# Stick-breaking heads of an encoder layer: the strict mask as one more TensorE product per query block, and |z| on ScalarE

## The chip, the cores and the metric

The kernel runs on one core of one Trainium2 chip. The metric is the device time of one execution in microseconds (us). The engines of the core are named as the profile names them: PE (TensorE matmul), PEld (TensorE weight load), DVE (VectorE), ACT (ScalarE), POOL (GpSimd) and SP (SyncE, which only issues transfers here).

## What is computed

One encoder layer on 512 tokens of width 2048: a norm, one projection to queries, keys and values of three groups of attention heads, the three kinds of attention, an output projection with a residual, then a gated MLP with a short causal convolution, a second residual and a last norm. The change touches the second group only, eight stick-breaking heads of width 64:

```python
z = jnp.einsum('bhqd,bhkd->bhqk', q_blk, k).astype(jnp.float32) * scale
causal = k_pos[None, :] < q_pos[:, None]
log_1m_beta = jnp.where(causal, -jax.nn.softplus(z), 0.0)
suffix = lax.cumsum(log_1m_beta, axis=3, reverse=True) - log_1m_beta
log_a = jax.nn.log_sigmoid(z) + suffix
a = jnp.where(causal, jnp.exp(log_a), 0.0).astype(v.dtype)
return jnp.einsum('bhqk,bhkd->bhqd', a, v)
```

So both the softplus and the weight of a key at or after the query have to come out as zero.

## The kernel before, in words

**Tiling.** Tokens stand in four blocks of 128. Every fp32 operand of a large product is split into a high and a low part of type fp32r (a cast on ACT, line 59, and a subtraction on DVE, line 60), and a product is three matmuls (`mm3`, lines 63 to 66). Weights come in units of 128 x 2048 through SP, are split in halves of 128 x 1024, and the halves live in three buffers (`wspl`), so that the cast of a new half waits until PE has read the old one.

**Heads.** There are sixteen head steps n = 0 to 15: n = 0 to 7 are differential heads, n = 8 to 11 are pairs of stick-breaking heads (`stick_pair`), n = 12 to 15 are pairs of band heads. `weave` (line 608) writes PE's order by hand: it lets the head step n yield small pieces and puts between them the matmuls of `following(n)`, which are the projections of the next head (`project_head`, banks q and k) and part of the values of a later one (`values_unit`, bank v). PE runs in exactly that order. The order on ACT, DVE and POOL is chosen by a planner, once, when the kernel is built; on the chip each engine then works its list strictly in order.

**A stick pair before the change** (lines 513 to 557). For each of the two heads c = 0, 1: four query blocks i = 3, 2, 1, 0 of scores, each from two matmuls into a PSUM bank (`block_scores`, lines 352 to 358), copied by ACT into z (line 536; a tile of 128 x 1280 that holds the four blocks' lower triangle, with the diagonal block last in each). Then a chain over that tile, in which every step needs the one before:

- line 540, DVE: l = min(-z, z), which is -|z|
- lines 541 and 542, ACT: l = exp(l), then l = ln(1 + l)
- line 543, DVE: l = max(z, 0) + l, the softplus
- line 518 with l, POOL: in each of the four diagonal blocks, l = 0 where the key is not before the query
- line 548, DVE: four scans from the right, one per query block
- line 549, DVE: z = z - l
- line 518 with z, POOL: z = -3e38 in the same places
- line 551, ACT: z = exp(z)

After both heads the generator yields `SB_WAIT` = 28 units, so that PE gets that much of the other matmuls. Then PE transposes the first head's z (line 388, tile `tr`), ACT and DVE split the transposes into rh and rl (lines 59 and 60), the same follows for the second head, and the products with the values (lines 402 and 403, bank `pv`) and the head norm end the step.

**Temporaries.** Bias tiles of the differential and the band heads share two buffers (tag `bias`): `dist` takes the first and serves until head step 7; `rbias` (line 493, loaded by POOL's queue) takes them in turn for the band heads. Other temporaries of 128 x 512 share six buffers (tag `t2`).

Of the kernel before, what the change touches and what calls it, by code (L numbers as in the profile page):

```python
# [8 lines left out]
F32 = mybir.dt.float32  # L9
F32R = mybir.dt.float32r  # L10
AF = mybir.ActivationFunctionType
ALU = mybir.AluOpType
# [3 lines left out]
P = 128  # L16
S = 512
D = 2048
KT = D // P
NB = S // P  # L20
# [3 lines left out]
NCH = NFT // CH  # L24
NSEV = 32
NEG = -3.0e38
SB_WAIT = 28
NORM_EPS = 1e-6
SUBLN_EPS = 1e-5
# [13 lines left out]
def trunk(ctx, tc, xT, wqkv, wo, wo15, wgu, wd, par, lam4, rel, out):  # L43
    nc = tc.nc
    sync, act, dve, pool, pe = nc.sync, nc.scalar, nc.vector, nc.gpsimd, nc.tensor
# [37 lines left out]
    def acc_bank(name="acc"):  # L83
        return ps_acc.tile([P, S], F32, tag="acc", name=name)

    def att_bank(name="att"):
        return ps_att.tile([P, S], F32, tag="att", name=name)
# [42 lines left out]
    ident = const.tile([P, P], F32, name="ident")  # L130
# [80 lines left out]
    def constants(tmp, khigh):  # L211
# [11 lines left out]
        dve.scalar_tensor_tensor(out=dist, in0=dist, scalar=-1.0, in1=dist, op0=ALU.mult, op1=ALU.min)  # L223
        dve.memset(dist[0:HD, S - HD : S], NEG)
        scr = tmp.tile([P, S], F32, tag="t2", name="scr")
# [15 lines left out]
    with ExitStack() as actx:  # L241
        qk = actx.enter_context(tc.tile_pool(name="qk", bufs=2))
        vp = actx.enter_context(tc.tile_pool(name="vp", bufs=4))
        tmp = actx.enter_context(tc.tile_pool(name="tmp", bufs=6))
# [104 lines left out]
            return (p[:, 0 : 2 * P], 2) if j == NB - 1 else (p[:, PAD + OFF[j] : PAD + OFF[j] + WID[j]], j)  # L349


        def block_scores(qkh, c, i, bank):


            q, k, kh = qkh
            qt, kt = slice(i * P, (i + 1) * P), slice(0, max(i + 1, 2) * P)
            pe.matmul(bank[:, kt], q[c][:, qt], k[c][:, kt], start=True, stop=False)  # L357
            pe.matmul(bank[:, kt], q[c][:, qt], kh[c][:, kt], start=False, stop=True)  # L358

        UOFF = [0, 128, 384, 768]  # L360

        def softmax_block(qkh, c, i, bias, dst, sums, n):
# [11 lines left out]
                scale=1.0,  # L374
                scalar=NEG,
                accum_out=mx,
# [4 lines left out]
        def transposed(w):  # L381

            (ph, pl), p = parts()
            for j in reversed(range(NB)):
                bank = att_bank("tr")
                for i in range(j, NB):
                    o = UOFF[i] + j * P
                    pe.transpose(out=bank[:, (i - j) * P : (i - j + 1) * P], in_=w[:, o : o + P], identity=ident)  # L388
                t = slice(OFF[j], OFF[j] + WID[j])
                split(ph[:, t], pl[:, t], bank[:, 0 : WID[j]])  # L390
                yield 1
            return p
# [87 lines left out]
        def pair_out(vs, p0, p1, gain, slot):  # L480
            v = vs()
            o, ct = o_tile(), tmp.tile([P, S], F32, tag="t2", name="ct")
            values_pair(0, v, p0, ct, o)
            yield 2
            values_pair(1, v, p1, ct, o)
            yield 1
            yield from finish(o, pair1, HD, NORM_EPS, gain, slot)

        def chunk_pair(p, qkh, vs):
            ws = []  # L490
            for c in range(2):
                bias = tmp.tile([P, S], F32, tag="bias", name="rbias", bufs=2)
                pool.dma_start(bias, rel[2 * p + c])
                dve.memset(bias[0:HD, S - HD : S], NEG)
                w = f5.tile([P, TRI], F32, tag="f5", name="w")
# [15 lines left out]
            yield from pair_out(vs, p0, p1, pt[:, C_CH + p : C_CH + p + 1], 12 + p)  # L511

        def stick_pair(p, qkh, vs):
            def strictly_before(t, fill):

                for i in range(NB):
                    o = UOFF[i] + i * P
                    pool.affine_select(  # L518
                        out=t[:, o : o + P],
                        in_=t[:, o : o + P],  # L520
                        pattern=[[-1, P]],
                        compare_op=ALU.is_gt,
                        fill=fill,
                        base=0,
                        channel_multiplier=1,
                    )

            zs = []
            for c in range(2):
                z = f5.tile([P, TRI], F32, tag="f5", name="z")  # L530
                zs.append(z)
                for i in reversed(range(NB)):
                    w = (i + 1) * P
                    bank = att_bank("z")
                    block_scores(qkh, c, i, bank)
                    act.copy(out=z[:, UOFF[i] : UOFF[i] + w], in_=bank[:, 0:w])
                    yield 1

                l = f5.tile([P, TRI], F32, tag="f5", name="l")
                dve.scalar_tensor_tensor(out=l, in0=z, scalar=-1.0, in1=z, op0=ALU.mult, op1=ALU.min)  # L540
                act.activation(l, l, AF.Exp)
                act.activation(l, l, AF.Ln, bias=1.0)
                dve.scalar_tensor_tensor(out=l, in0=z, scalar=0.0, in1=l, op0=ALU.max, op1=ALU.add)
                strictly_before(l, 0.0)
                for i in reversed(range(NB)):

                    back = l[:, UOFF[i] : UOFF[i] + (i + 1) * P][:, ::-1]
                    dve.tensor_tensor_scan(back, back, back, 0.0, ALU.add, ALU.max)  # L548
                dve.tensor_tensor(out=z, in0=z, in1=l, op=ALU.subtract)
                strictly_before(z, NEG)  # L550
                act.activation(z, z, AF.Exp)
            yield SB_WAIT
            p0 = yield from transposed(zs[0])
            yield 6
            p1 = yield from transposed(zs[1])
            yield 1
            yield from pair_out(vs, p0, p1, pt[:, C_SB + p : C_SB + p + 1], 8 + p)


        TOTAL = {diff_head: 30, stick_pair: 33 + SB_WAIT, chunk_pair: 39}  # L560
        NH, HEADS_AT = 16, 16
        ready, vtiles, pending = {}, {}, []

        def unit_order():
            yield from (HEADS_AT, HEADS_AT + 1)
# [23 lines left out]
        def nxt():  # L589

            load_next()
            return ahead.pop(0)
# [5 lines left out]
        def following(n):  # L598

            yield from project_head(n + 1, nxt)  # L600
            m, s = (n + 2) // 2, n % 2
            if s == 0:
                vbanks[:] = [acc_bank("v0"), acc_bank("v1")]
            yield from values_unit(m, s, vbanks, nxt())
            if s == 1:
                vtiles[m] = values_out(m, vbanks)

        def weave(n, others, count, lead=0, slack=0, last=True):
            att, total = head(n)
            done, emitted = 0, lead  # L610
            for _ in range(lead):
                next(others)
            for w in att:
                done += w
                while emitted < count and (emitted - lead) * (total + slack) < done * (count - lead):
                    emitted += 1
                    next(others, None)
            for _ in others if last else ():
                pass
# [46 lines left out]
        input_scale_columns()  # L666
        vtiles[0] = values_out(0, vbanks)
        for n in range(NH - 2):
            weave(n, following(n), 48, 8 if n == 0 else 0)
        last = first_outputs()  # L670
        weave(NH - 2, last, 46, last=False)
# [14 lines left out]
    with ExitStack() as actx:  # L686
# [19 lines left out]
        for m in range(KT):  # L706
            if m < 4:
                bank = wo_banks[m]
            else:
                bank = acc_bank("wo")  # L710
# [277 lines left out]
    with ExitStack() as actx:  # L988
# [237 lines left out]
        with tc.manual_schedule(engines={E.PE, E.DVE, E.Activation, E.SP, E.Pool}):  # L1226
# [4 lines left out]
            for s in range(len(units) * NSTEP + 3):  # L1231
                u, k = divmod(s, NSTEP)
                if u < len(units):
                    v, q = divmod(s + 1, NSTEP)
# [166 lines left out]
```

## Time and profile before

| | us |
|---|---|
| median of three timed runs | 2220.88 (2220.15 to 2222.6) |
| the profiled execution, its own time | 2223.95 |
| its span, first to last instruction | 2222.2 |
| PE busy in the span | 2176.9 (98%) |
| PEld / DVE / ACT / POOL busy | 1984.2 / 1614.7 / 1060.1 / 324.1 |
| stretch of the four stick pairs | 375 to 555 |

The profile is one execution. Its first part gives the busy time of each engine. A view by windows gives the same for stretches of the span, with the clock granted to TensorE as a share of 2.4 GHz. A view of waits says which instruction sat idle until which other ended. A timeline lists instructions by engine with their start and length, and in brackets the idle time before them and what ended it. A busy PE is not a PE at its peak, since matmuls overlap; what one matmul costs is read from the start of it to the start of the next.

### The profile page before, as it was taken

Reading aid. Unit: us, or ns where it says so; the run is one execution under the profiler, and the core shown is the slowest. Engines: PE = TensorE matmul, PEld = TensorE weight load, DVE = VectorE, ACT = ScalarE, POOL = GpSimd, SP = SyncE. Lnnn points to the kernel's source line nnn. Section 1 sums busy time; section 2 is a strip of 40 time slices with the busy share of each in tenths; the row PEclk is TensorE's granted clock in tenths of the full one; section 3 lists DMA queues with packets and bytes.
Section 4 is the critical chain, followed back from the end, with each engine's and each line's share of the span. In section 5 each row is a group of like instructions: output and inputs, shape, how many; then the busy total and the mean of one; then the engine's idle time right before and its main releaser. Section 6 shows DMA issues by size and latency. Waiting matters only on the chain.

```text
span 2222.2 us, 34979 instructions
## 1 busy us (share of the span) xinstructions
PE 2176.9 (98%) x13884; PEld 1984.2 (89%) x13884; DVE 1614.7 (73%) x2283; ACT 1060.1 (48%) x1558; POOL 324.1 (15%) x593
## 2 busy tenths in 40 slices
PE   8999999989999999989999999999999999999997
PEld 7889898878888888889999999999999978888887
DVE  6665666787777546877777777777777778887675
ACT  5555555565566333344444444444444554544232
POOL 0100101221110321112111111111111110000003
PEclk9999999999999999999999999999999999999999
DMA  5332434222234544778778877787777565655742
GB/s 199 104 115 100 123 101 125 84 80 76 86 117 141 187 145 164 257 233 242 196 218 220 211 222 221 191 239 217 195 187 205 206 235 194 213 199 220 273 170 77
DMA packets 98164, 388.15 MB, mean 175 GB/s; under 512 B 11408, under 2 KB 20368, under 8 KB 81040
## 3 DMA queue, kind: packets, MB, share of 16 engines
q1 hardware_dynamic: 65728, 269.90, 35.7%
q0 software_dynamic: 30976, 114.84, 20.2%
q8 instruction: 109, 1.79, 0.3%
q10 hardware_dynamic: 1296, 1.17, 0.2%
q14 instruction: 55, 0.45, 0.1%
HBM read 341.30 MB, written 52.95 MB: 177 GB/s over the span
## 4 chain that ended last, share of the span: by engine, by line
PE 87%; DVE 5%; DMA 3%; ACT 2%; issue 2%; POOL 1%; SPq 0%; POOLq 0%; DVEq 0%; ACTq 0%
PE c L66 36%; PE r L66 12%; PE wo L66 8%; PE v L66 8%; PE q L66 6%; PE k L66 6%; PE dn L66 6%; PE tr L388 1%; DMA f<-t_dram 1%; PE pv L66 1%; PE sc L358 1%; PE sc L357 1%; DVE l L548 1%; POOL z L518 1%; DMA xt<-x_dram 1%
## 5 line engine op out<-in xcount | busy, mean ns | idle before, releaser
L60 DVE TENSOR_TENSOR wl<-a,wh 128x1024 fp32r<-128x1024 f32 x199 | 243.4, 1223 | 176.2 <-ACT wh L59 176.0
L66 PE MATMUL c<-bl,wh 128*128 128x256 f32 x1280 | 363.6, 284 | 4.7 <-ACT wh L59 4.7
L66 PE MATMUL c<-bh,wl 128*128 128x256 f32 x1280 | 363.5, 284 | 2.3 <-DVE wl L60 2.3
L66 PE MATMUL c<-bh,wh 128*128 128x256 f32 x1280 | 363.3, 284 | 0.0
L59 ACT CAST wh<-a 128x1024 fp32r<-128x1024 f32 x199 | 209.0, 1050 | 243.4 <-DVE a L862 206.6
L59 ACT CAST wh<-raw 128x1024 fp32r<-128x1024 f32 (+1 forms) x163 | 168.6, 1035 | 257.4 <-PE wo L66 85.1
L66 PE MATMUL c<-h2l,wh 128*128 128x256 f32 x960 | 272.0, 283 | 1.4 <-DVE U L888 0.9
L66 PE MATMUL c<-h2h,wl 128*128 128x256 f32 x960 | 271.8, 283 | 0.0
L66 PE MATMUL c<-h2h,wh 128*128 128x256 f32 x960 | 271.8, 283 | 0.0
L66 PEld LDWEIGHTS c<-bl,wh 128*128 128x128 f32 x1280 | 246.9, 193 | 4.9 <-ACT wh L59 4.9
L66 PEld LDWEIGHTS c<-bh,wl 128*128 128x128 f32 x1280 | 246.8, 193 | 2.6 <-DVE wl L60 2.6
L66 PEld LDWEIGHTS c<-bh,wh 128*128 128x128 f32 x1280 | 246.8, 193 | 0.0
L60 DVE TENSOR_TENSOR wl<-raw,wh 128x1024 fp32r<-128x1024 f32 (+1 forms) x163 | 197.6, 1214 | 65.6 <-ACT wh L59 64.9
L66 PEld LDWEIGHTS c<-h2l,wh 128*128 128x128 f32 x960 | 184.4, 192 | 1.8 <-DVE U L888 1.1
L66 PEld LDWEIGHTS c<-h2h,wl 128*128 128x128 f32 x960 | 184.4, 192 | 0.0
L66 PEld LDWEIGHTS c<-h2h,wh 128*128 128x128 f32 x960 | 184.4, 192 | 0.0
L66 PE MATMUL r<-wl,fh 128*128 128x512 f32 x448 | 174.8, 390 | 2.3 <-DVE wl L1129 2.3
L66 PE MATMUL r<-wh,fh 128*128 128x512 f32 x448 | 174.4, 389 | 0.0
L66 PE MATMUL r<-wh,fl 128*128 128x512 f32 x448 | 174.3, 389 | 0.0
L66 PE MATMUL v<-wl,hh 128*128 128x256 f32 x512 | 149.3, 292 | 9.5 <-DVE wl L60 9.2
L66 PE MATMUL v<-wh,hl 128*128 128x256 f32 x512 | 147.2, 287 | 0.4 <-DVE hl L170 0.4
L66 PE MATMUL v<-wh,hh 128*128 128x256 f32 x512 | 147.0, 287 | 0.0
(301 smaller groups left out, 5204.9 us busy)
## 6 DMA issues: line engine op xcount, KB each, us to landing
a<-in_wgu SPq DMA_DIRECT2D x121, 512.0 KB, 5.9
raw<-in_wd SPq DMA_DIRECT2D x48, 1024.0 KB, 5.8
raw<-in_wqkv SPq DMA_DIRECT2D x46, 1024.0 KB, 4.8
z<-in_wgu SPq DMA_DIRECT2D x80, 512.0 KB, 5.5
z<-in_wgu POOLq DMA_DIRECT2D x78, 512.0 KB, 9.5
raw<-in_wo SPq DMA_DIRECT2D x16, 1024.0 KB, 4.8
raw<-in_wgu SPq DMA_DIRECT2D x8, 1024.0 KB, 4.8
ab_dram<-g POOLq DMA_DIRECT2D x32, 256.0 KB, 6.3
```

Source lines behind the costliest of these rows:

```text
L59: a = act.copy(out=hi, in_=src)
L60: d = dve.tensor_tensor(out=lo, in0=src, in1=hi.bitcast(F32), op=ALU.subtract)
L66: pe.matmul(o, l[x], r[y], start=start and i == 0, stop=stop and i == 2, skip_group_check=on)
L357: pe.matmul(bank[:, kt], q[c][:, qt], k[c][:, kt], start=True, stop=False)
L358: pe.matmul(bank[:, kt], q[c][:, qt], kh[c][:, kt], start=False, stop=True)
L388: pe.transpose(out=bank[:, (i - j) * P : (i - j + 1) * P], in_=w[:, o : o + P], identity=ident)
L518: pool.affine_select(out=t[:, o : o + P], in_=t[:, o : o + P], pattern=[[-1, P]], compare_op=ALU.is_gt, fill=fill, base=0, channel_multipl ...
L548: dve.tensor_tensor_scan(back, back, back, 0.0, ALU.add, ALU.max)
```

## The change

The mask is made once, before head step 7 (`far_masks`): a 128 x 128 identity and a 128 x 256 tile whose left half is zero and whose right half holds -2^127 where the key is not before the query, both in fp32r. `block_scores` gets a third matmul for the stick heads, identity times mask, which adds the mask to the last 256 columns of the block's scores (128 columns for block 0). A masked score is then about -1.7e38: its |z| gives exp(-|z|) = 0, ln(1 + 0) = 0 and max(z, 0) = 0, so its softplus is 0, and exp(z - l) is 0. The two POOL selections per head (`strictly_before`) go. -|z| on DVE becomes |z| on ACT, and the minus moves into the scale of the exponential.

```diff
+FAR = -(2.0**127)
...
-        def block_scores(qkh, c, i, bank):
+        def block_scores(qkh, c, i, bank, strict=False):
...
             pe.matmul(bank[:, kt], q[c][:, qt], k[c][:, kt], start=True, stop=False)
-            pe.matmul(bank[:, kt], q[c][:, qt], kh[c][:, kt], start=False, stop=True)
+            pe.matmul(bank[:, kt], q[c][:, qt], kh[c][:, kt], start=False, stop=not strict)
+            if strict:
+
+                w = P if i == 0 else 2 * P
+                kt = slice((i + 1) * P - w, (i + 1) * P)
+                pe.matmul(bank[:, kt], far[0], far[1][:, 2 * P - w :], start=False, stop=True)
...
-            def strictly_before(t, fill):
-
-                for i in range(NB):
-                    o = UOFF[i] + i * P
-                    pool.affine_select(
-                        out=t[:, o : o + P],
...
-                block_scores(qkh, c, i, bank)
+                block_scores(qkh, c, i, bank, True)
...
-                dve.scalar_tensor_tensor(out=l, in0=z, scalar=-1.0, in1=z, op0=ALU.mult, op1=ALU.min)
-                act.activation(l, l, AF.Exp)
+                act.activation(l, z, AF.Abs)
+                act.activation(l, l, AF.Exp, scale=-1.0)
                 act.activation(l, l, AF.Ln, bias=1.0)
                 dve.scalar_tensor_tensor(out=l, in0=z, scalar=0.0, in1=l, op0=ALU.max, op1=ALU.add)
-                strictly_before(l, 0.0)
...
                 dve.tensor_tensor(out=z, in0=z, in1=l, op=ALU.subtract)
-                strictly_before(z, NEG)
                 act.activation(z, z, AF.Exp)
...
+        def far_masks():
+
+            t = tmp.tile([P, S], F32R, tag="bias", name="far", bufs=2)
+            b = tmp.tile([P, S], F32, tag="t2", name="diagonal")
+            pool.memset(b[:, 0 : 2 * P], 0.0)
+            pool.affine_select(
+                out=b[:, P : 2 * P],
+                in_=b[:, P : 2 * P],
+                pattern=[[-1, P]],
+                compare_op=ALU.is_gt,
+                fill=FAR,
+                base=0,
+                channel_multiplier=1,
+            )
+            dve.tensor_copy(t[:, 0:P], ident)
+            dve.tensor_copy(t[:, P : 3 * P], b[:, 0 : 2 * P])
+            far[:] = t[:, 0:P], t[:, P : 3 * P]
...
         for n in range(NH - 2):
+            if n == 7:
+                far_masks()
             weave(n, following(n), 48, 8 if n == 0 else 0)
```

## Rows read from the trace of the kernel before

**Rows 1.** First part of the page: busy us (share of the span) x instructions.

```profile
PE 2176.9 (98%) x13884; PEld 1984.2 (89%) x13884; DVE 1614.7 (73%) x2283; ACT 1060.1 (48%) x1558; POOL 324.1 (15%) x593
```

**Rows 2.** Windows: stretch, length, busy us of each engine (instructions), granted clock, DMA, GB/s.

```profile
375.00:555.00 180.00, 168.21 (x962) 147.63 (x962) 140.98 (x195) 110.47 (x193) 40.42 (x89) 0.97 0.25 82
555.00:665.00 110.00, 110.00 (x636) 96.33 (x635) 79.89 (x209) 66.84 (x153) 15.75 (x41) 1.00 0.28 98
880.00:955.00 75.00, 68.05 (x321) 57.03 (x320) 62.83 (x94) 31.25 (x35) 7.93 (x15) 0.96 0.82 268
```

**Rows 3.** Waits within 375 to 556: total us, times, longest.

```profile
ACT z L551 <- POOL z L518: 35.0, 8, 8.5
...
PE tr L388 <- ACT z L551: 10.0, 4, 2.8
...
PE pv L402 <- DVE rl L60: 1.1, 1, 1.1
```

**Rows 4.** Timeline of PE: start, us, instruction, idle time before it and its releaser.

```profile
400.36 0.33 PE L388 MATMUL tr<-ident,z 128*128 128x128 f32 x1 [2.15 <-ACT z L551]
...
452.51 0.55 PE L388 MATMUL tr<-ident,z 128*128 128x128 f32 x3 [2.81 <-ACT z L551]
...
490.84 0.33 PE L388 MATMUL tr<-ident,z 128*128 128x128 f32 x1 [2.22 <-ACT z L551]
...
543.61 0.90 PE L388 MATMUL tr<-ident,z 128*128 128x128 f32 x3 [2.81 <-ACT z L551]
```

**Rows 5.** Windows around the last two of these, columns as in the second group.

```profile
491.50:495.50 4.00, 4.00 (x17) 3.35 (x16) 3.40 (x5) 2.99 (x7) 1.97 (x4) 0.57 0.02 4
542.50:550.00 7.50, 6.39 (x31) 6.39 (x32) 5.69 (x10) 6.76 (x13) 0.00 (x0) 0.54 0.33 128
```

**Rows 6.** Timeline of DVE, POOL and ACT: end of the chain, head step 8, c = 0.

```profile
393.70 1.49 DVE L549 TENSOR_TENSOR z<-z,l 128x1280 f32<-128x1280 f32 x1
...
396.03 2.97 POOL L518 TENSOR_SCALAR_AFFINE_SELECT z<-z 128x128 f32<-128x128 f32 x4
...
399.03 1.27 ACT L551 ACTIVATE z<-z 128x1280 f32<-128x1280 f32 x1 [8.42 <-POOL z L518]
```

**Rows 7.** The same timelines: head step 9, chain of c = 1, and a weight cast.

```profile
433.99 1.05 ACT L59 CAST wh<-raw 128x1024 fp32r<-128x1024 f32 x1 [4.23 <-PE q L66]
...
439.65 1.57 DVE L543 SCALAR_TENSOR_TENSOR l<-z,l 128x1280 f32<-128x1280 f32 x1
...
443.92 2.97 DVE L548 TENSOR_TENSOR_SCAN l<-l 128x512 f32<-128x512 f32 x4
...
447.64 1.49 DVE L549 TENSOR_TENSOR z<-z,l 128x1280 f32<-128x1280 f32 x1
...
449.26 1.89 POOL L518 TENSOR_SCALAR_AFFINE_SELECT z<-z 128x128 f32<-128x128 f32 x4 [6.89 <-DVE z L549]
...
451.19 1.27 ACT L551 ACTIVATE z<-z 128x1280 f32<-128x1280 f32 x1 [5.85 <-POOL z L518]
```

**Rows 8.** Line 540: engine, operation, times, ns min/median/max, first and last start.

```profile
L540 DVE SCALAR_TENSOR_TENSOR l<-z x8: 1465/1484/1492, 381.3 to 526.2; 128x1280 f32<-128x1280 f32 x8
```

**Rows 9.** Timeline of PE in the scores of head step 8.

```profile
377.72 0.28 PE L357 MATMUL z<-a,a 128*128 128x256 f32 x1
...
377.96 0.39 PE L66 MATMUL q<-hl,wh 128*128 128x512 f32 x1
378.19 0.40 PE L66 MATMUL q<-hh,wl 128*128 128x512 f32 x1
```

**Rows 10.** The last score product of the stick heads, and a later reader of `rbias`.

```profile
L358 PE MATMUL z<-kh,a x32: 279/311/400, 375.8 to 517.9; 128*128 128x256 f32 x16, 128*128 128x512 f32 x8, 128*128 128x384 f32 x8
...
569.89 0.69 DVE L368 CUSTOM_DVE_ANT_0 w<-sc,rbias 128x512 f32<-128x512 f32 x1
```

**Rows 11.** A product whose operands are both full fp32 (timeline of PE).

```profile
864.13 1.02 PE L779 MATMUL ssq<-ssum,ones_r 128*128 128x512 f32 x2
```

**Rows 12.** A table load, from the groups of ACT: count, busy us, mean ns.

```profile
L741 ACT ACT_TABLE_LOAD x1 | 1.3, 1283 | 0.0
```

More of the change, by code (lines that the diff above doesn't have):

```diff
@@ L513, in stick_pair @@
         def stick_pair(p, qkh, vs):
-            def strictly_before(t, fill):
-                for i in range(NB):
-                    o = UOFF[i] + i * P
-                    pool.affine_select(
-                        out=t[:, o : o + P],
[L520 to L526, printed above, removed]
             zs = []
@@ L561, in trunk @@
         NH, HEADS_AT = 16, 16
-        ready, vtiles, pending = {}, {}, []
+        ready, vtiles, pending, far = {}, {}, [], []
+        def far_masks():
[14 more added lines that the diff above has]
+            far[:] = t[:, 0:P], t[:, P : 3 * P]
         def unit_order():
```

## The prediction

> **What bounds the kernel now.** I read the first part of the page first: PE is busy 98% of the span [rows 1], so an edit off PE gains only where PE stands still, and an edit on PE costs its full length elsewhere. Next, the windows: in the stretch of the four stick pairs PE is busy 168.21 of 180.00 us, in the 110 us behind it 110.00 of 110.00 [rows 2]. The stick pairs thus hold 180.00 - 168.21 = 11.8 us of standing PE, and that is all there is to win by shortening their chain. Third, the waits of that stretch, for what ends this idle time: 10.0 us in four waits are transposes that wait for the last exponential (line 551); one wait of 1.1 us is a value product waiting for the low part of a transpose, work that comes after that same exponential; the rest (0.7) is a weight half. And line 551 itself was held 35.0 us in eight waits by the POOL selection ahead of it [rows 3]. The PE timeline places the four: one for each pair, 2.15 and 2.22 us at the first head (c = 0) of steps 8 and 10, 2.81 and 2.81 us at the second head (c = 1) of steps 9 and 11 [rows 4]. Last, the granted clock just behind the last two stalls: 0.57 over 4.00 us and 0.54 over 7.50 us [rows 5], where 1.00 is the rule. At the level 1.2 GHz PE does half the work, so this is a second loss that the stalls bring.
>
> **The change part by part.**
>
> *The selection on z goes.* At c = 0 of step 8 the subtraction ends at 393.70 + 1.49 = 395.19, the selection runs from 396.03 to 399.00, and the exponential starts at 399.03 [rows 6]. Without it the exponential could start at about 395.3, 3.7 us sooner, for a stall of 2.15. At c = 1 of step 9 the subtraction ends at 447.64 + 1.49 = 449.13 and the exponential starts at 451.19 [rows 7]: 2.0 us for a stall of 2.81. This alone leaves 0.8 there.
>
> *The selection on l goes.* At c = 1 of step 9 the softplus is ready at 439.65 + 1.57 = 441.22, but the scans start at 443.92 [rows 7], 2.7 us later. What lies between is POOL's selection and a DVE instruction that stood behind the c = 0 exponential, which POOL had also held. With both gone up to 2.7 us more come free; 2.0 + 2.7 = 4.7 against a stall of 2.81.
>
> *|z| moves from DVE to ACT.* DVE loses eight instructions of 1.484 us [rows 8]; ACT gains eight over the same 1280 columns, for which its exponential takes 1.27 [rows 7]. No row shows an absolute value, so I take 1.27; the ends are 1.27 and the DVE's 1.48. In length the chain gains 0.2 us. But ACT must now do three steps in a row in its strict order, among score copies and casts. Bounds: nothing lost, or one more ACT instruction ahead of it, about 1.3 us per head; I take 1.3. Then the margins are 3.7 - 1.3 - 2.15 = 0.25 us for the first kind of stall and 4.7 - 1.3 - 2.81 = 0.6 for the second. In both cases the mask products ahead of the transposes (eight a pair, next paragraph) also let PE arrive about 1 us later, so the margins are 1.2 and 1.6 us. ACT is busy 110.47 of 180.00 us in the stretch and gains 8 x 1.27 = 10.2 [rows 2]: two thirds busy, no bound. For scale, the Trainium skill ("ScalarE: Activation LUTs", Rules for kernel authors) says that max, min, add and mul belong on VectorE and not on ScalarE, which speaks against this move. The rows of this case say otherwise for an fp32 tile of 1280 columns: 1.27 us on ACT, 1.48 on DVE; by the skill's rule the chain would lose a little instead of gaining 0.2, which the margins would cover.
>
> *The mask products.* 2 heads x 4 blocks x 4 pairs = 32 matmuls, 24 of 256 columns and 8 of 128. In the scores two products of 256 columns take 377.96 - 377.72 = 0.24 us from start to start, 0.12 each; one of 512 columns takes 378.19 - 377.96 = 0.23 [rows 9]. The 256 columns make 24 x 0.12 = 2.9 us. For 128 columns in fp32r no row stands; it is between 0.06 (half of 0.12) and 0.23 (as 512 columns), and I take 0.12, as for the nearest shape: 8 x 0.12 = 1.0. Together 3.8 us, from 3.4 to 4.7. They stand where PE has no idle time, so nothing hides them, and a gain is excluded: PE does the same work and these besides.
>
> *The masks themselves, and the moved buffers.* One POOL memset, one selection, two DVE copies of at most 256 columns, once, around head step 7, in which PE does not wait. I cost them at nothing; if a DVE job behind them were waited for, at about 1 us, once. `far` takes one of the two `bias` buffers until the last stick scores, which end near 518 [rows 10]; the second bias tile of step 12 can then be loaded by POOL's queue only after that. The readers of the bias come late (one at 569.89, [rows 10]), some 50 us behind. POOL has at that point nothing queued that PE needs at once, since its selections are gone.
>
> *The stalls go, and what is late next.* With the margins above I expect all four transposes to find their data. Behind them the weight half and the low part of a transpose are next in line; both had been pushed back by the late exponential in ACT's order. I keep 0.7 us, one wait of the shortest kind, as a remainder: 11.8 - 0.7 = 11.1 us gained.
>
> *The clock.* Behind two of the four stalls PE ran at half rate: 4.00 x (1 - 0.57) = 1.7 us lost, and 6.39 busy us x (1 - 0.54) = 2.9 [rows 5]; 4.7 us, paid back if the stalls go. Bounds: 0 (if it fell anyway) and twice this (if all four stalls had set it off). The stretch behind, without idle time and with the same kind of transposes, has 1.00 throughout [rows 2], so I take 4.7. The Trainium skill ("TensorE: Matmul & The Clock Gate", Part 1) says that the default state is throttled, that activity releases it, and that the same kernel can meet the gate differently from run to run. The rows fit: a stall of 2.81 us had a drop behind it in step 11 and none in step 9. By that rule alone the 4.7 could be anything from 0 to 9 in a timed run.
>
> *The sum.* -11.1 - 4.7 + 3.8 = -12.0 us. For the profiled execution, 2223.95 - 12.0 = 2211.95. It stands 3.1 us above the median of the timed runs; I carry the difference over unchanged: 2220.88 - 12.0 = 2208.9. I see nothing behind the stretch that would give it back: the next 110 us are PE's own, and the one place with much DMA, 880 to 955 at a share of 0.82 [rows 2], starts from sums that PE's results release, so it moves with them. The loss of clock there (0.96) could change by a few us either way as things shift.
>
> **The rivals.**
>
> *Half the stalls stay.* The planner's new order on ACT may put a weight cast ahead of |z| or of the last exponential. For: such casts wait up to 4.23 us in order for PE to read an old half [rows 7], and my margins are 1.2 and 1.6 us. Against: at step 9 that very wait already stands inside the c = 1 chain and is counted. Half of everything: -5.9 - 2.3 + 3.8 = -4.4, 2216.5.
>
> *The mask product costs what full fp32 costs.* A product of full fp32 operands of 512 columns shows as two matmuls and 1.02 us [rows 11]; half of that for 256 columns would be 24 x 0.5 + 8 x 0.25 = 14 us. Then -15.8 + 14 = -1.8, 2219. Against: both operands are declared fp32r, like those of the scores.
>
> *|z| needs other tables.* Were a table load of 1.28 us [rows 12] needed before and after each |z|, the chain would gain 2.6 us a head: 2.6 over margins of 1.2 and 1.6 leaves stalls of 1.4 and 1.0, in all 4.8 us; -7.0 - 2.3 + 3.8 = -5.5, 2215.4. Against: in the attention copies, squares, Exp and Ln alternate today without a load between; the next load is that of line 741, in the MLP [rows 12]. The skill's ScalarE page (section Table sets) counts abs among the functions in every set; no row here shows it.
>
> *Slower: ACT's list is blocked at the last exponential.* If in every pair the cast that waits for PE (4.23, and 1.05 for itself) is put ahead of the c = 0 exponential, that head gives up its 3.7 us gain for a loss of 5.3 and comes 1.6 later than now, while the second head's stall stays: 4 x (2.15 + 1.6) + 2 x 2.81 = 20.6 us of idle time instead of 11.8, +8.8 + 3.8 = +12.6, 2233. It decides from where the idle time left exceeds 11.8 - 3.8 = 8.0 us at an unchanged clock. For: the planner fills ACT by its own costs, not by PE's true progress. Against: ACT stood idle 8.42 us before that exponential [rows 6] and no cast was put there.
>
> **How the numbers follow.** A measurement of this kernel tells about 0.2% (4.4 us) from no change. Forecast, 2208.9: 0.74; its own range 2204.2 (clock term at twice 4.7) to 2212.1 (clock term at one half, mask at 4.7). Half the stalls: 0.13, split evenly about the 0.2% line at 2216.5. Other tables: 0.03, just on the faster side, two to one. Full fp32 mask: 0.03, same. Slower: 0.06. A planner accident elsewhere that cancels out: 0.01, same. Faster 0.74 + 0.06 + 0.02 = 0.82; same 0.07 + 0.01 + 0.03 + 0.01 = 0.12; slower 0.06. The range goes from 2204.2 to 2217, past the middle of the first rival.
>
> **What would show it.** Right: in the stretch of the stick pairs no PE idle time before the transposes of z, granted clock 1.00, a stretch shorter by about 12 us, the mask products 0.12 apart, no wait of line 551 for POOL. Wrong: transposes still waiting for line 551, now behind an ACT cast; mask products 0.4 us apart or more; table loads in the stretch; or the stretch shorter by 12 us and the end not.

## The result, and the profile after

| | before | after |
|---|---|---|
| median of the timed runs, us | 2221.07 (2220.15 to 2222.6) | 2206.52 (2204.97 to 2207.37) |
| the profiled execution, its own time | 2223.95 | 2206.56 |
| span | 2222.2 | 2204.8 |
| stick stretch | 488.60 | 474.15 |

The ratio is 0.9933, with a 95% interval of 0.9916 to 0.9950: faster by 14.55 us, where 12.0 were forecast. The stick stretch is here, and below, the time from the start of the first score product of step 8 to the start of the norm-sum product of the gated MLP (line 779 before, 790 after): 864.13 - 375.53 before, 848.02 - 373.87 after. It takes in the four stick pairs and all that follows up to the MLP; from the first score of step 12 to its end it lasts 305.68 us before and 305.70 after, so the whole difference arose in the stick pairs. It fell by 14.45 us, so the gain of the timed runs was made there and nothing behind it gave any back. The profiled spans differ by more, 17.4 us; where the other 3 come from is the first experiment's matter.

First part of the page of the changed kernel; it answers to [rows 1]:

```profile
PE 2173.9 (99%) x13916; PEld 1984.3 (90%) x13916; DVE 1604.0 (73%) x2277; ACT 1071.9 (49%) x1566; POOL 292.5 (13%) x531
```

PE has 32 instructions more, POOL 62 fewer (64 selections gone, two instructions for the mask added), ACT eight more. Now the windows of the four stick pairs, from the first score of one step to that of the next; columns as in [rows 2]:

```profile
373.87:415.98 42.11, 42.11 (x256) 37.66 (x254) 34.03 (x54) 31.52 (x58) 2.50 (x7) 1.00 0.39 111
415.98:458.09 42.11, 42.11 (x255) 37.65 (x254) 31.29 (x40) 29.83 (x46) 1.61 (x6) 1.00 0.24 82
458.09:500.21 42.12, 42.12 (x256) 37.66 (x255) 34.03 (x54) 31.53 (x58) 1.56 (x6) 1.00 0.23 82
500.21:542.32 42.11, 42.11 (x256) 37.64 (x254) 31.33 (x41) 29.84 (x46) 2.10 (x7) 1.00 0.25 88
```

PE is busy in all of it, at the full clock, and all four steps take the same 42.11 us. Before, 11.8 us of 180 were idle and the clock was 0.97 [rows 2]. The timeline of ACT and PE at the place of [rows 6], both heads of step 8:

```profile
391.09 1.27 ACT L542 ACTIVATE z<-z 128x1280 f32<-128x1280 f32 x1
...
400.16 1.28 ACT L542 ACTIVATE z<-z 128x1280 f32<-128x1280 f32 x1 [5.14 <-DVE z L541]
```

```profile
397.18 0.28 PE L395 MATMUL tr<-ident,z 128*128 128x128 f32 x1
...
403.96 0.49 PE L395 MATMUL tr<-ident,z 128*128 128x128 f32 x3
```

The last exponential (line 542 now) ends at 392.36 and 401.44; PE comes for them at 397.18 and 403.96. So the chain now has 4.8 us to spare at the first head (c = 0) and 2.5 at the second (c = 1). In step 9 it is 6.1 and 5.7, in the same way; steps 10 and 11 repeat 8 and 9. The mask products on PE, beside [rows 9]:

```profile
374.10 0.39 PE L360 MATMUL z<-kh,a 128*128 128x512 f32 x1
374.33 0.28 PE L365 MATMUL z<-far 128*128 128x256 f32 x1
374.45 0.40 PE L67 MATMUL q<-hl,wh 128*128 128x512 f32 x1
...
377.58 0.22 PE L365 MATMUL z<-far 128*128 128x128 f32 x1
377.64 0.45 PE L67 MATMUL q<-hl,wh 128*128 128x512 f32 x1
377.93 0.39 PE L67 MATMUL q<-hh,wl 128*128 128x512 f32 x1
```

One of 256 columns takes 0.12 from start to start. One of 128 takes 0.06, but the product behind it then takes 0.29 instead of 0.23, so it costs 0.12 too. 32 x 0.12 = 3.84 us, the value forecast. The mask itself was made by one copy of 0.221 us and one of 0.295 on DVE, one of them in the start-up and one in step 7, with no wait of PE. The load of the second bias tile waits on POOL's queue 1.5 us for the last mask product, at 508, 45 us before it is first read (553.76), so this wait costs nothing. The table loads are the three that were there.

### The profile page after: what moved, and what is told of

Same layout as the page of the kernel before. It is cut to its first block, busy times and chain, and to the rows that moved or that the text cites. A ratio compares the mean times of both kernels' runs of the same rounds, so it can differ in the third digit from the quotient of the medians.

```text
span 2204.8 us, 34927 instructions
## 1 busy us (share of the span) xinstructions
PE 2173.9 (99%) x13916; PEld 1984.3 (90%) x13916; DVE 1604.0 (73%) x2277; ACT 1071.9 (49%) x1566; POOL 292.5 (13%) x531
## 4 chain that ended last, share of the span: by engine, by line
PE 95%; DMA 2%; DVE 2%; issue 1%; ACT 0%; SPq 0%; DVEq 0%; POOLq 0%; ACTq 0%
PE c L67 36%; PE r L67 12%; PE v L67 8%; PE q L67 8%; PE k L67 8%; PE wo L67 8%; PE dn L67 6%; PE g L67 2%; PE u L67 2%; PE tr L395 1%; DMA f<-t_dram 1%; PE pv L67 1%; PE sc L360 1%; PE sc L359 1%; PE pv L410 0%
```

## The experiments

All times stand against 2220.4 to 2221.1 for the kernel before, the medians on the chips of those runs (2219.64 for the last experiment), and 2206.5 to 2206.8 for the changed kernel. The stick stretch is from the profiled execution of each.

| kernel | time, us | ratio to before (95%) | stick stretch | PE stalled or slowed in it |
|---|---|---|---|---|
| before | 2221.07 | 1 | 488.60 | 18.3 |
| before again | 2218.48, one execution | | 487.23 | 16.9 |
| before + mask products | 2224.09 | 1.0017 (1.0007 to 1.0026) | 491.30 | 17.2 |
| before + abs on ACT | 2216.22 | 0.9978 (0.9968 to 0.9987) | 482.98 | 12.7 |
| before, SB_WAIT 44 | 2226.09 | 1.0023 (1.0013 to 1.0032) | 493.44 | 23.1 |
| after + selection on z | 2213.77 | 0.9972 (0.9963 to 0.9982) | 480.73 | 6.6 |
| after + selection on l | 2208.75 | 0.9947 (0.9932 to 0.9962) | 475.82 | 1.7 |
| after, abs on DVE | 2209.35 | 0.9950 (0.9935 to 0.9965) | 475.53 | 1.4 |
| after, no mask | 2203.04 | 0.9921 (0.9906 to 0.9935) | 470.72 | 0.4 |
| after, mask on DVE | 2217.25 | 0.9980 (0.9970 to 0.9990) | 484.25 | 13.9 |
| after, early POOL mask | 2211.59 | 0.9958 (0.9943 to 0.9973) | 477.42 | 7.1 |
| after again | 2206.82 | 0.9942 (0.9927 to 0.9957) | 474.15 | 0 |
| mixed mask | 2205.00 | 0.9932 (0.9918 to 0.9946) | 473.39 | 2.1 |

The last column is the stretch less what PE needs for it without a pause: 474.15 with the 32 products, as the changed kernel shows, and, by 0.12 us for each product that is not made, 470.31 without them and 471.27 with eight. The kernel without the mask shows no wait and 470.72, so the worked-out values are good to about 0.4 us. The stretch is of one execution each, and the two profiles of the kernel before differ by 1.4 us in it, so where a kernel is set against it below, both differences are given.

**Two controls.** The kernel before, and the changed one, profiled once more.

> The kernel before, unchanged, profiled once more. From its first profile to that of the changed kernel the stick stretch (first score of step 8 to the norm sum at line 779) fell by 14.45 us (488.60 to 474.15), but the span fell by 17.4: the start-up was 1.7 us shorter and the passage to the gated MLP about 1.6 us. Theory: only the 14.45 belong to the change, and the other 3 us are differences between two executions. Then this profile shows the same four stalls (2.2, 2.8, 2.2, 2.8 us), a stick stretch of 488.6 within 1 us unless the clock falls elsewhere, and a start-up (first score of step 8) anywhere from 373.8 to 375.6. Rival: the planner's new order in the changed kernel also made the start-up shorter; then this run has its first score at 375.5 again.

> The changed kernel, unchanged, beside the run above on the same chip. Theory: 2206.5 within 1.5; stick stretch 474.15 within 0.3 us (no stall, no fall of the clock, so nothing in it can vary), while start-up and the passage to the gated MLP may differ by 1 to 2 us. Rival: the 17.4 us by which the profiled spans differed are all the change's; then the span is 2204.8 within 0.5 again and the start-up the same.

The stretch of the changed kernel came out at 474.15 to the hundredth, although the start-up was 1.2 us longer (first score at 375.10). The kernel before has the same four stalls, 10.0 us in total, but its first score stands at 373.99 where it was 375.53, and its span is 2216.8 where it was 2222.2. So start-up differs by 1.5 us between two executions of the kernel before and by 1.2 between two of the changed one, and what stands behind the norm sum (1358.1 and 1355.6 us; 1356.8 and 1359.7) by 2.5 and 2.9. The surplus of 3 us between the two profiled spans, 1.7 in front of the stretch and 1.3 behind it, is no more than that. The clock behind the last two stalls, beside [rows 5], in the second profile of the kernel before:

```profile
490.00:495.00 5.00, 5.00 (x25) 4.28 (x24) 4.40 (x8) 3.99 (x9) 1.97 (x4) 0.66 0.02 5
540.00:545.00 5.00, 2.99 (x14) 2.99 (x15) 2.94 (x5) 3.88 (x6) 0.65 (x3) 0.68 0.63 211
545.00:550.00 5.00, 5.00 (x39) 4.82 (x38) 4.27 (x8) 4.57 (x9) 0.36 (x2) 0.98 0.00 0
```

It fell again behind the same two stalls, but the second fall was nearly over by 545, while the first profile, whose step 11 starts 1.6 us later, has 0.54 over the whole of 542.5 to 550 [rows 5]. The stretch is 1.4 us shorter, and 1.3 of that lies in step 11 (45.79 us against 47.11): the same stalls cost less by the clock in this execution.

**The mask products alone.**

```diff
 # before
-                    block_scores(qkh, c, i, bank)
+                    block_scores(qkh, c, i, bank, True)
```

> The kernel before with the mask products added, both POOL selections and -|z| on DVE kept. Theory: 32 products cost 0.12 us each, 3.84 in all, on an engine without idle time at that place; at the first heads of steps 8 and 10 PE then comes 0.96 us later to transposes whose chain starts 0.48 later, so those two stalls shrink by 0.48 each: 3.84 - 0.96 = +2.9, 2224 against 2221. Rival: the products are hidden in the stalls that follow, since PE only waits there anyway: +0 to +0.5, 2221.

Measured: 3.25 us more in the timed runs (2224.09 against 2220.84), 2.7 in the stretch against the first profile of the kernel before and 4.1 against the second. The products are not hidden in the stalls. The forecast 2.9 is borne out as a number, but not by its sum: the two stalls did not just shrink by 0.48 each. PE's waits in the stick pairs add up to 11.7 us, as before (11.8), and stand elsewhere: 0.9 at the first and 2.8 at the second heads of steps 8 and 10, 1.35 at the first heads of steps 9 and 11. So one half of the change, made alone, would have been a loss, clear of its interval.

**No mask.**

```diff
 # after
-                    block_scores(qkh, c, i, bank, True)
+                    block_scores(qkh, c, i, bank)
```

> The changed kernel without the mask products; the strict mask is left out altogether. Theory: the chain ends 2.5 to 6.1 us before PE reaches the transposes, so PE stays without idle time and the 3.84 us of products come off whole: 2206.5 - 3.8 = 2202.7. Rival: part of the products lies beside other waits of PE (weight loads, bank releases) and less comes off: 2204.5 to 2206.5. A second rival: PE, arriving up to 1 us sooner, meets stalls again: idle time before line 395.

Measured: 2203.04, 3.5 below the changed kernel, and 3.43 in the stretch, without any PE wait in it. So the price of the mask comes out near 3.84 from the other side too. (The ratios of the two kernels overlap; this reading rests on the stretch.)

**One selection put back.**

```diff
 # after, first kernel: on l behind the softplus; second kernel: on z behind the subtraction
+                strictly_before(l, 0.0)
...
+                strictly_before(z, NEG)
```

> The changed kernel with the POOL selection on l put back (a redundant one, the mask products stay). The chain ends 4.8, 2.5, 6.1 and 5.7 us ahead of PE in the four kinds of head (steps 8 and 10: c = 0, c = 1; steps 9 and 11: c = 0, c = 1). Theory: only the chain's length against these margins counts; the selection adds 1 to 1.6 us, under all four margins: no stall, 2206.5 within 1. Rival: it is POOL in the chain as such, by the turn-taking of two heads on ACT and DVE, that brings the stalls: some of the four come back, 2209 to 2214.

> The changed kernel with the POOL selection on z put back (redundant too). Theory: it adds 2.0 to 3.8 us, as at steps 9 and 8 before; margins 4.8 and 2.5 in steps 8 and 10, 6.1 and 5.7 in 9 and 11: at most the c = 1 heads of steps 8 and 10 stall, by up to 1.3 us each: 2206.5 to 2209.5. Rival: the selection on z holds ACT's list and with it the weight casts, as the 35.0 us of waits of line 551 suggested; then stalls before the transposes and before weight halves come back and the clock falls: 2212 or more.

The selection on l costs 1.7 us in the stretch, 1.4 of it in steps 8 and 10, where value products wait a little (0.9 us shown as idle); no transposes wait. Its ratio overlaps that of the changed kernel, so these 1.7 rest on the stretch. The selection on z costs 6.6, 3.3 in each of steps 8 and 10 (45.41 us against 42.11), nothing in 9 and 11. Transposes of the second head wait again, but longer than the added 1.9 us of POOL explain at a margin of 2.5. The timelines of POOL, ACT, DVE and PE in step 8 show why:

```profile
389.94 3.26 POOL L525 TENSOR_SCALAR_AFFINE_SELECT z<-z 128x128 f32<-128x128 f32 x4 [10.06 <-DVE z L555]
401.09 1.89 POOL L525 TENSOR_SCALAR_AFFINE_SELECT z<-z 128x128 f32<-128x128 f32 x4 [7.88 <-DVE z L555]
```

```profile
393.23 1.27 ACT L557 ACTIVATE z<-z 128x1280 f32<-128x1280 f32 x1 [3.49 <-POOL z L525]
394.41 0.60 ACT L322 CAST a<-f 64x512 fp32r<-64x512 f32 x1
...
403.01 1.27 ACT L557 ACTIVATE z<-z 128x1280 f32<-128x1280 f32 x1 [6.12 <-POOL z L525]
```

```profile
395.05 0.69 DVE L337 TENSOR_TENSOR a<-f,a 64x512 fp32r<-64x512 f32 x1 [2.00 <-ACT a L322]
395.75 2.97 DVE L554 TENSOR_TENSOR_SCAN l<-l 128x512 f32<-128x512 f32 x4
```

```profile
404.33 0.33 PE L395 MATMUL tr<-ident,z 128*128 128x128 f32 x1 [1.47 <-ACT z L557]
```

The selection of the first head (c = 0) holds ACT's list at line 557 until 393.23. The cast of the next queries (line 322) stands behind it, a DVE subtraction (line 337) behind that cast, and the scans of the second head (c = 1) behind that subtraction, 2.00 us late. So one head's selection is paid by the other head as well. The expectation, which set the chain's length alone against the margins, was too low (2206.5 to 2209.5). 2213.8 lies where the rival had it, and ACT's list was indeed held; but what came late behind it was the cast of the queries and not a weight half, and the clock did not fall.

**|z| put back on DVE, and |z| moved alone.**

```diff
 # after, first kernel (the second is the reverse, made in the kernel before)
-                act.activation(l, z, AF.Abs)
-                act.activation(l, l, AF.Exp, scale=-1.0)
+                dve.scalar_tensor_tensor(out=l, in0=z, scalar=-1.0, in1=z, op0=ALU.mult, op1=ALU.min)
+                act.activation(l, l, AF.Exp)
```

> The changed kernel with -|z| on DVE again, as before. Theory: the step is 0.2 us longer and queued on DVE; margins of 2.5 and more cover it, no stall: 2206.5 within 1, so the move of |z| to ACT gave nothing. Rival: DVE's order (two heads, scans, weight halves) was the true hold-up and the move to ACT a part of the gain: stalls come back, 2209 or more.

> The kernel before with |z| on ACT alone (selections kept, no mask products). Theory: the stalls end at the POOL selections, which stay; the chain gets 0.2 us shorter at the start and ACT fuller: the four stalls within 1 us of 2.2, 2.8, 2.2, 2.8, time 2221 within 3. Rival: the move frees DVE for the scans and takes most of the stalls away: 2212 or less.

In the changed kernel the move is worth 1.4 us of the stretch (2.5 to 2.8 in the timed runs, where the ratios overlap). The last exponential and the first transposes of both heads of step 8, with |z| on DVE:

```profile
392.36 1.26 ACT L542 ACTIVATE z<-z 128x1280 f32<-128x1280 f32 x1
...
400.35 1.28 ACT L542 ACTIVATE z<-z 128x1280 f32<-128x1280 f32 x1 [2.81 <-DVE z L541]
```

```profile
395.49 0.28 PE L395 MATMUL tr<-ident,z 128*128 128x128 f32 x1
...
402.28 0.49 PE L395 MATMUL tr<-ident,z 128*128 128x128 f32 x3
```

The chains have 1.9 and 0.65 us to spare here, where the changed kernel has 4.8 and 2.5; in step 9 it is 3.2 and 4.3 where it was 6.1 and 5.7. So the move gave the four heads 1.4 to 3.0 us each. In the kernel before, alone, it is worth 4.5 us in the timed runs and 5.6 in the stretch (4.3 against the second profile), where I had expected nothing. The waits of PE in the stick stretch of that kernel:

```profile
PE pv L402 <- DVE rl L60: 3.7, 4, 1.1
PE tr L388 <- ACT z L551: 3.7, 4, 1.1
PE v L66 <- DVE wl L60: 2.4, 2, 1.2
```

The transposes wait 3.7 us instead of 10.0 [rows 3], the granted clock is 1.00 throughout, and the waits behind them have grown. Step 9 shows the reason, first before on DVE, then with the move on ACT and DVE:

```profile
435.12 1.47 DVE L540 SCALAR_TENSOR_TENSOR l<-z 128x1280 f32<-128x1280 f32 x1
```

```profile
428.37 1.28 ACT L540 ACTIVATE l<-z 128x1280 f32<-128x1280 f32 x1
...
434.96 1.48 DVE L543 SCALAR_TENSOR_TENSOR l<-z,l 128x1280 f32<-128x1280 f32 x1
```

On DVE the |z| of the second head stood behind the scans of the first, until 435.12. On ACT it runs at 428.37, and the softplus (line 543) starts at 434.96 instead of 439.65 [rows 7]: 4.7 us earlier, of which 1.6 are the earlier start of the whole step.

**The stalls avoided by PE's order.**

```diff
 # before
-SB_WAIT = 28
+SB_WAIT = 44
```

> The kernel before with SB_WAIT = 44 instead of 28, nothing else: PE does more of the other matmuls ahead of the transposes of z. By the share of pieces (52 of 77 instead of 36 of 61 ahead of the first head's, 62 of 77 instead of 46 of 61 ahead of the second's, 48 pieces of about 0.7 us) PE comes 2.9 us later to the first head's transposes and 1.7 us later to the second's. Theory: the chain is untouched and only its end against PE's arrival counts: the stalls of 2.2 go, those of 2.8 fall to about 1.1, the clock no longer falls: -(2 x 2.5 + 2 x 1.7 + 4) = about -12, 2209, without a mask product. Rival: the wait moves on to the value products, which then stand closer behind the transposes (line 402 waiting for rl): 2215 to 2221.

Measured: slower by 5.7 us. No transposes wait for line 551 any more, and yet PE stands still longer. PE, with the idle time ahead of products of bank v (the next values) in steps 8 and 10, and then ACT in step 8:

```profile
405.14 0.58 PE L66 MATMUL v<-wl,hh 128*128 128x256 f32 x1 [3.71 <-DVE wl L60]
...
499.20 0.58 PE L66 MATMUL v<-wl,hh 128*128 128x256 f32 x1 [4.43 <-DVE wl L60]
```

```profile
399.67 1.28 ACT L551 ACTIVATE z<-z 128x1280 f32<-128x1280 f32 x1 [8.02 <-POOL z L518]
400.85 1.03 ACT L59 CAST wh<-raw 128x1024 fp32r<-128x1024 f32 x1
```

What PE waits for is a weight half whose cast stands directly behind line 551 in ACT's list, and line 551 stood 8.02 us at the head of that list. Neither of the two outcomes I had written down came: the wait moved on, but to the weights and not to the value products. The clock fell too, to a mean of 0.96, 0.96 and 0.93 in steps 8 to 10.

**The mask on DVE.**

```diff
 # after; far[0] is the mask as fp32
-                    block_scores(qkh, c, i, bank, True)
-                    act.copy(out=z[:, UOFF[i] : UOFF[i] + w], in_=bank[:, 0:w])
+                    block_scores(qkh, c, i, bank)
+                    o = UOFF[i] + i * P
+                    if i:
+                        act.copy(out=z[:, UOFF[i] : o], in_=bank[:, 0 : i * P])
+                    dve.tensor_tensor(out=z[:, o : o + P], in0=bank[:, i * P : w], in1=far[0], op=ALU.add)
```

> The changed kernel with the mask added by DVE instead of PE: DVE adds the mask tile to the diagonal block while it copies it out of PSUM (32 additions of 128 x 128), and ACT copies only the columns left of it. Theory: PE is rid of 3.84 us, and DVE, busy 130 of 168 us in the stretch, takes 32 x 0.3 = 10 us more; the chain grows by less than 1 us a head against margins of 2.5 to 6.1, so nothing of it shows: 2202.7, below both kernels. Rival: DVE's strict order puts the additions behind weight halves and the scores' banks come free late: stalls at the scores or the transposes, 2205 to 2212.

The rival came, and worse. The additions run late in DVE's list, the PSUM banks of the scores come free late, and PE stands at the very scores of steps 8 and 10:

```profile
379.13 0.47 PE L359 MATMUL z<-a,a 128*128 128x512 f32 x1 [2.04 <-DVE z L532]
```

Four waits of transposes for line 545 (the last exponential here), 4.7 us in all, 3.8 of it in the same two steps, and a mean clock of 0.96 in these come on top.

**The mask on POOL, but early.**

```diff
 # after, in place of the products and of far_masks
                     act.copy(out=z[:, UOFF[i] : UOFF[i] + w], in_=bank[:, 0:w])
+                    pool.affine_select(out=z[:, o : o + P], in_=z[:, o : o + P], ..., fill=FAR, ...)
```

> The changed kernel with the mask put back on POOL, but at the head of the chain: POOL writes -2^127 into the diagonal block of z as soon as ACT has copied that block's scores; no mask products, no selection later, |z| on ACT. Theory: only the last of the four selections of a head, about 0.3 us with its wait, lies in the chain, and one selection alone does not hold ACT or DVE the way those behind DVE's results did; against margins of 2.5 to 6.1 us no stall, and PE is rid of 3.84 us: 2202.7, as without any mask. Rival: any use of POOL within the chain brings order and waits back: ACT's |z| waits for POOL at the head of its list, casts behind it are late, stalls as with the mask on DVE: 2206.5 to 2217.

Half of each came. Steps 9 and 11 take 41.19 us, without a stall and without products, 0.92 less than in the changed kernel. Steps 8 and 10 stall by 2.33 and 2.37 us at the second head and last 45.45 and 43.89; in step 8 the clock fell as well (a mean of 0.96, against 1.00 in step 10). POOL and DVE of step 8, and a selection of step 9:

```profile
386.23 4.00 POOL L531 TENSOR_SCALAR_AFFINE_SELECT z<-z 128x128 f32<-128x128 f32 x4 [4.87 <-ACT z L529]
```

```profile
387.40 3.10 DVE L550 TENSOR_TENSOR_SCAN l<-l 128x512 f32<-128x512 f32 x4
```

```profile
427.15 0.29 POOL L531 TENSOR_SCALAR_AFFINE_SELECT z<-z 128x128 f32<-128x128 f32 x1 [0.81 <-ACT z L529]
```

In step 8 the four selections of the second head fall together with the softplus step and the scans of the first (from 387.40) and take 4.00 us, and ACT's |z| waits for the last of them; a selection that runs while DVE stands idle takes 0.29.

**Both kinds of mask.**

```diff
 # after, with the early selection where no product is made
+                    product = c == 1 and p % 2 == 0
+                    block_scores(qkh, c, i, bank, product)
```

> The changed kernel with the early POOL selection in six of the eight heads of the stick pairs and the mask products only in the second head of steps 8 and 10, where the early selection had stalled PE by 2.3 us. Theory: with 8 products instead of 32, 24 x 0.12 = 2.9 us come off PE, and the selections that coincide with the first head's scans are gone, so no stall is left: stick stretch 474.15 - 2.9 = 471.3, time 2206.7 - 2.9 = 2203.8, below both kernels. Rival: the planner lays ACT's and DVE's lists out anew, as with the mask on DVE, and a stall comes back somewhere: stretch 473 or more, 2206 or more.

Measured: 2205.00 (2201.94 to 2206.18), with no PE wait in the stick pairs, but a stretch of 473.39 instead of 471.3: steps 8 and 10 take 42.12 and 42.10 us (first score to first score) instead of the 41.6 that four products a step would make, and about a microsecond more goes between step 11 and the MLP. The pauses are too short to show as waits, but the starts show them: in step 8 the first score of the second head (376.27) takes 0.35 us to the next start instead of 0.23, and around the first value product (405.80 to 406.50) 0.36 and 0.34 go where 0.12 and 0.23 are the rule, as DVE makes the low parts of the transposes only from 405.81 on. The microsecond is mostly one wait of 0.83 us in a band head: transposes at 683.57 wait for a low part made on DVE. So the rival's stretch came (473 or more), though not its time. Its ratio, 0.9932 (0.9918 to 0.9946), overlaps that of the changed kernel beside it (0.9942, 0.9927 to 0.9957). Whether it is faster than the changed kernel isn't settled.

## Why the prediction was right, and what was off in it

**What bounds the kernel: right.** The gain was made where PE stood still, and only there: 14.45 us in the stretch, 14.55 in the timed runs.

**The mask products: right.** 3.84 us by the rows; 3.4 to 3.5 come off without them.

**The stalls and the clock: right in kind, wrong in size, and the two errors partly cancel.** The forecast took 11.8 us of idle time, left 0.7 and gained 11.1, and added 4.7 for the clock. Steps 8 and 10 do the same work in the same order, and so do 9 and 11, and at an unchanged clock such a pair lasts equally long: 44.86 and 44.95, 43.74 and 43.74 in the kernel with |z| moved alone. In the kernel before, the clock fell in 10 and 11 only. That separates the two terms. The four steps of the kernel before, by windows:

```profile
375.53:420.24 44.71, 41.83 (x247) 36.50 (x246) 36.93 (x56) 28.95 (x56) 11.13 (x23) 1.00 0.36 105
420.24:465.94 45.70, 41.82 (x247) 36.72 (x246) 33.92 (x42) 27.01 (x44) 9.60 (x22) 1.00 0.21 75
465.94:511.34 45.40, 43.18 (x247) 37.91 (x246) 37.09 (x56) 29.07 (x56) 10.12 (x22) 0.96 0.21 76
511.34:558.45 47.11, 44.30 (x247) 39.41 (x246) 34.01 (x42) 27.00 (x44) 9.57 (x22) 0.93 0.21 73
```

Without a pause a step needs 42.11 - 8 x 0.12 = 41.15. At the clock 1.00, steps 8 and 9 lost 3.56 and 4.55. Steps 10 and 11 lost 4.25 and 5.96, which is 0.7 and 1.4 more. So of the 18.3 us lost the stalls cost 2 x (3.56 + 4.55) = 16.2, where the forecast had 11.1, and the clock 2.1, where it had 4.7 (in the second profile 0.7: 0.61 and 0.10). -16.2 - 2.1 + 3.8 = -14.5.

Why the stalls cost more than their idle time: the number in brackets is counted from the modelled end of the product before, but without a wait the next one would have started before that end. The stall of 2.81 in step 9 follows a product that starts at 449.43 and lasts 0.28, while such products follow each other 0.12 apart; the transposes start at 452.51, so 2.96 us are lost. The same 0.16 or so is missing at each of the other waits in steps 8 and 9. Together with pauses of 0.11 that show no wait this accounts for most of what those steps lost.

Why the clock cost less than the work that it withheld: a slower PE comes later to what it would have waited for anyway. Step 8 has a second wait, 0.74 us for a weight half, and step 9 one of 1.08 for a low part; steps 10 and 11 have neither. I had added the idle time and the clock as if they were independent. It is not always so small: in the kernel with the early selection, step 8, where the clock fell, lasted 1.56 us longer than step 10 with the same stall. That the total came within 2.5 us of the forecast is thus in part luck. Against the second profile of the kernel before, the stretch fell by 13.1 us and not 14.45.

The Trainium skill ("TensorE: Matmul & The Clock Gate", Part 1) says that the same kernel can meet the gate differently from run to run; the two profiles of the kernel before agree (0.54 from 545 to 550 in the first, 0.98 in the second).

**The margins: wrong in size, from a wrong step.** I gave the two heads that stalled 1.2 and 1.6 us to spare; they have 4.8 (first head of steps 8 and 10) and 5.7 (second head of steps 9 and 11). The tightest is one that I had not worked out, the second head of steps 8 and 10, with 2.5. The step that failed is "|z| moves from DVE to ACT": I charged it 1.3 us and credited 0.2, and it is a gain. With |z| on DVE in the otherwise changed kernel the same two heads have 1.9 and 4.3, so it gave them 3.0 and 1.4. Made alone it took 4.3 to 5.6 us off the stretch, since it takes an instruction out of DVE's list that stood behind the other head's scans. I had priced the instruction and not its place. The Trainium skill's rule for max, min, add and mul ("ScalarE: Activation LUTs", Rules for kernel authors), whose factor is given for bf16, doesn't hold for this |z| in fp32: 1.28 us on ACT, 1.48 on DVE, and 4.5 us of the timed runs.

**The selections: the one on z mattered most.** Put back, it alone costs 6.6 us of the stretch, the one on l 1.7. I had counted the selection on z with its own head (3.7 and 2.0 us) and seen in the row of line 336 only its echo on the other head; that echo is as large as the direct effect: in step 8 of the experiment 1.9 us of POOL at the second head, and 2.0 by which its scans start late.

**The rivals.** Half the stalls stay, full fp32 rate, other tables: none came. "ACT's list is blocked at the last exponential" didn't come either. Its reverse is real: not a cast ahead of the exponential but one behind it. In the kernel with SB_WAIT 44 a weight cast behind line 551, which waits for POOL, stops PE by 3.71 and 4.43 us. Before the change the cast stood there too (at 400.21, directly behind line 551), mostly covered by the stall of the transposes; that the 0.7 us which I kept as a remainder was its visible end fits the order of the instructions, but no run tested it. Had the change moved the transposes instead of shortening the chain, this would have been next in line, which I didn't name at its true size.

**What stays open.** Whether the mixed mask is faster than the changed kernel, and why the clock fell behind the stalls of steps 10 and 11 and not behind those of 8 and 9. The parts are also not additive: |z| on ACT is worth 4.3 to 5.6 us of the stretch beside the selections and 1.4 without them, so no split of the 14.5 among the parts is given.

## What to carry to other kernels

When an engine with a strict list waits at its head, price not only the waiting chain but everything queued behind it, on that engine and on the engines that wait for those; moving one short elementwise step to another engine's list can be worth more than its length (here a step of 1.48 us moved, and the softplus of that head came 3.1 us sooner). Before adding work to the bound engine in order to shorten a chain, check that the stall it removes exceeds the work added: here 16.9 to 18.3 us against 3.84, while the same products without the rest were a loss of 3 us. And do not simply add the idle time and the lost clock: a slower engine waits less afterwards. Delaying the consumer is no substitute for shortening the chain if the same waiting instruction also holds the next things that the consumer needs.

## What the runs showed of the hardware

A selection of 128 x 128 on POOL takes 0.29 us by itself, and four of them took 4.00 us, 1.0 each, beside a DVE softplus step and DVE scans, which read two operands from SBUF. The Trainium skill ("SBUF — State Buffer", SBUF: two separate sides) says that GpSimd and a DVE instruction with two SBUF inputs lock each other out for a whole instruction. POOL's side of the rows agrees; DVE lost next to nothing by it (3.10 us for the four scans, 2.97 with POOL idle [rows 7]).

A product of 128 fp32r columns took 0.06 us from start to start, but made the product behind it 0.06 longer, so nothing was gained by halving 256 columns (377.58 in the changed kernel, and so at all eight of them).
